# Loading a 268 MB matrix in tiles of 512 rows and three slots, instead of 384 rows and four slots

## The chip, the cores and the metric

The kernel runs on one core of one Trainium2 chip. The metric is the time of one execution on the device, in microseconds (us), the median of several executions. The kernel before takes 631.39 us (4 runs, 631.29 to 631.71). The runs come in batches; all kernels of one batch run on the same chip, each beside runs of the kernel before. The batches fell on different chips, and there the kernel before has medians between 631.36 and 632.11 us, so a kernel is compared with the runs of before of its own batch, or with a kernel of the same batch.

## The reference

```python
B, S, D = 8, 2048, 4096
proj = (x @ w).squeeze(-1)                 # x: (8, 2048, 4096) float32, w: (4096, 1)
cm = np.maximum.accumulate(proj, axis=1)
is_record = (proj >= cm).astype(np.float32)
return np.cumsum(is_record, axis=1).astype(np.float32)
```

One pass over x, 268.4 MB, decides everything. Each row of 4096 numbers (16 KB) becomes one dot product; a running maximum and a running count follow along each of the 8 sequences.

## The kernel before

Five groups of 384 positions are processed in a loop, and then one tail of 128 positions. In a group, each of the 8 sequences is one tile: 128 partitions with three consecutive rows each, so a tile is one load with one contiguous run of 48 KB per partition. Four slots of SBUF hold tiles. The loads are all issued from SyncE (SP) in program order; a load waits until its slot's last tile has been released (`fr`, counted by VectorE and ScalarE).

```python
    R = 3          # rows per partition and tile
    NS = 4         # slots
    NG = (S - P) // (R * P)                      # 5 groups
    ...
        for k in range(NK):                      # NK = NG * B = 40 tiles
            g, t = divmod(k, B)
            i = SY.dma_start(
                out=xbuf[k % NS],
                in_=x[B - 1 - t, g * N : (g + 1) * N, :].rearrange(
                    "(p r) d -> p (r d)", r=R
                ),
            ).then_inc(xs[k % NS], 16)
            if k >= NS:
                i._wait_ge(fr[k % NS], 2 * (k // NS))
```

Every row is split over three engines: VectorE multiplies and sums columns 0 to 2815 in one instruction, GpSimd (POOL) multiplies the other 1280 columns in place, ScalarE (ACT) sums those. Small matmuls transpose a group's sums into PSUM, and VectorE then runs three instructions over the group's positions: running maximum, comparison, running count.

```python
        with V.Fori(0, NG):                      # VectorE; POOL and ACT have the same loop
            group_scans()
            ...
            for t in range(B):
                b, s = B - 1 - t, t % NS
                V.wait_ge(xs[s], 16).then_inc(go, 1)
                V.sem_inc(xs[s], -16)
                for j in range(R):
                    i = dot(...)
                i.then_inc(fr[s], 1)
```

With four slots and eight tiles to a group, `k % NS` and `t % NS` are the same slot in every group. That is why the loop can be written once for all groups. The tail loads single 16 KB rows and, for the last sequences, narrow pieces.

## Time and profile before

| | before |
|---|---|
| time, median | 631.39 us |
| span of the profiled execution | 630.1 us |
| DMA, share of sixteen engines' span | 98.7% |
| VectorE, POOL, ACT busy | 64%, 59%, 28% |
| first load packet starts, last load has landed | 2.0 us, 623.57 us |

The page of the kernel before: the span; the DMA engines' mean busy share in tenths for forty slices; the DMA queues with packets, MB and share of sixteen engines' span; the engines on the chain that ended last; and the two costliest groups of instructions (busy us, mean ns of one, idle us before them and what ended it).

```profile
span 630.1 us, 1239 instructions
...
DMA  9999999999999999999999999999999999999995
...
q1 hardware_dynamic: 8016, 268.50, 98.7%
...
q14 instruction: 2, 0.02, 0.0%
...
POOL 52%; issue 38%; DMA 6%; PE 3%; DVE 0%; POOLq 0%; ACT 0%; SPq 0%; ACTq 0%
...
L120 DVE CUSTOM_DVE_ANT_0 xall<-xall,w_v 128x2816 f32<-128x2816 f32 (+3 forms) x135 | 389.3, 2931 | 185.8 <-DVEq L238 183.8
L252 POOL TENSOR_TENSOR xall<-xall,w_sb 128x1280 f32<-128x1280 f32 x120 | 345.2, 2903 | 246.0 <-POOLq L255 246.0
```

The chain is led by POOL and by "issue", but the last line shows POOL idle for 246.0 us: it waits for tiles. The limit is the load queue, in every slice but the last. The windows view of four tiles (columns: from and to, length, busy us of PE, PEld, DVE, ACT, POOL with counts, granted TensorE clock, DMA share, GB/s) says it best:

```profile
33.40:91.40 58.00, 0.00 (x0) 0.00 (x0) 36.45 (x24) 16.35 (x24) 34.51 (x12) 1.00 1.00 434
```

The DMA share is 1.00 and the rate 434 GB/s, while the busiest compute engine works 36.45 of 58.00 us. The Trainium skill, "DMA: Bandwidth & Descriptors", section Where 436 GB/s comes from, gives a ceiling of 435 GB/s for the sixteen DMA engines; this trace agrees. (The same section has the HBM side, at about 358 GB/s for a core, bind a load from HBM. Here this one core read at 434 GB/s, so that limit does not show, and the measurement decides.) So nothing that the compute engines do counts here, unless it makes the queue run dry.

`q14 instruction` are the fetches of the program itself.

The last three instructions of VectorE, in the timeline (start us, length us, instruction; in brackets the idle time before it and what ended that):

```profile
625.94 0.47 DVE L135 TENSOR_TENSOR_SCAN cm_l<-ps,cm,small 8x128 f32<-8x128 f32 x1 [1.70 <-PE ps L326]
626.45 0.28 DVE L139 TENSOR_TENSOR rec_l<-ps,cm_l 8x128 f32<-8x128 f32 x1
626.76 0.47 DVE L142 TENSOR_TENSOR_SCAN cnt_l<-rec_l,cnt,ps 8x128 f32<-8x128 f32 x1
```

More readings come from the trace's records and not from a view. A load's semaphore is counted up 16 times, which is read here as once by each DMA engine. The last of the 16 is called the landing here, and the time from the first to the last is the spread of the engines. In the kernel before, tiles land 14.50 us apart, tail rows 4.86 us apart, and the spread at the last landing is 1.36 us.

### The profile page before, as it was taken

To read this page: it belongs to the slowest core of one execution; us is meant where nothing else is said; L and a number is where in the kernel's file an instruction comes from. 1 tells how busy PE (TensorE), PEld (TensorE's weight loads), DVE (VectorE), ACT (ScalarE), POOL (GpSimd) and SP (SyncE) were. 2 spreads that over 40 slices of the span, in tenths; PEclk is the share of its full clock that TensorE was granted. 3 is DMA by queue.
4 is the path that set the end of the run, shared out by engine and by line. 5 is a ranking of instruction groups with operands and counts; after the bars stand their busy time and mean duration, and the time that the engine had idled before them with its cause. 6 is when DMAs were issued, how large, how long until landed. Compare 5 with 4: busy or idle time off the path is not lost.

```text
span 630.1 us, 1239 instructions
## 1 busy us (share of the span) xinstructions
PE 33.4 (5%) x100; PEld 14.7 (2%) x100; DVE 406.2 (64%) x295; ACT 177.7 (28%) x262; POOL 369.2 (59%) x137
## 2 busy tenths in 40 slices
PE   8000000010000001000000010000001000000103
PEld 3000000000000000000000000000000000000001
DVE  0756666677655557766666675556667766555886
ACT  1322223233232222233232322222232322322332
POOL 0555666666555555666666555556666665555864
PEclk9999999999999999999999999999999999999999
DMA  9999999999999999999999999999999999999995
GB/s 385 415 446 443 412 443 444 422 434 440 424 437 441 431 427 443 440 415 446 438 421 440 440 424 437 440 425 434 440 440 418 443 440 418 444 437 417 425 431 209
DMA packets 8035, 268.55 MB, mean 426 GB/s; under 512 B 936, under 2 KB 1496, under 8 KB 2016
## 3 DMA queue, kind: packets, MB, share of 16 engines
q1 hardware_dynamic: 8016, 268.50, 98.7%
q8 instruction: 1, 0.02, 0.0%
q10 hardware_dynamic: 16, 0.02, 0.0%
q14 instruction: 2, 0.02, 0.0%
HBM read 268.45 MB, written 0.07 MB: 426 GB/s over the span
## 4 chain that ended last, share of the span: by engine, by line
POOL 52%; issue 38%; DMA 6%; PE 3%; DVE 0%; POOLq 0%; ACT 0%; SPq 0%; ACTq 0%
POOL xall L252 52%; DMA xall<-in_x_dram 6%; PE w_v L206 2%; PE ps L326 1%; PE ps L206 0%; DMA w<-in_w_dram 0%; DVE xall L120 0%; POOLq L255 0%; ACT w L216 0%; DVE cm_l L135 0%; DVE cnt_l L142 0%; SPq L176 0%; DVE rec_l L139 0%; ACT xall L126 0%; POOLq L247 0%
## 5 line engine op out<-in xcount | busy, mean ns | idle before, releaser
L120 DVE CUSTOM_DVE_ANT_0 xall<-xall,w_v 128x2816 f32<-128x2816 f32 (+3 forms) x135 | 389.3, 2931 | 185.8 <-DVEq L238 183.8
L252 POOL TENSOR_TENSOR xall<-xall,w_sb 128x1280 f32<-128x1280 f32 x120 | 345.2, 2903 | 246.0 <-POOLq L255 246.0
L126 ACT ACTIVATE xall<-xall 128x1280 f32<-128x1280 f32 x129 | 162.6, 1261 | 430.9 <-POOL xall L252 413.1
L273 PE MATMUL ps<-identity,small 128*8 128x128 f32 x60 | 13.6, 418 | 567.1 <-ACT xall L126 567.1
L294 POOL TENSOR_TENSOR xall<-xall,w_sb 128x1280 f32<-128x1280 f32 (+1 forms) x8 | 22.1, 2765 | 6.7 <-DMA xall<-in_x_dram 6.6
L126 ACT ACTIVATION_READ_ACCUMULATOR xall<-xall 128x1 f32 x129 | 24.0, 186 | 0.0
L273 PEld LDWEIGHTS ps<-identity,small 128*8 128x8 f32 x60 | 7.4, 130 | 574.4 <-ACT xall L126 570.6
L135 DVE TENSOR_TENSOR_SCAN cm<-ps,cm,small 8x384 f32<-8x384 f32 x6 | 6.0, 1004 | 15.0 <-PE ps L273 15.0
L206 PE MATMUL w_v<-w,identity 8*128 8x512 f32 x14 | 12.1, 1056 | 0.0
L224 DVE MEMSET ps<- 8x384 f32 x1 | 0.4, 378 | 17.1 <-ACT w L216 17.1
L120 DVE DVE_READ_ACCUMULATOR2_ANT small<- 128x1 f32 x135 | 11.0, 81 | 0.0
L326 PE MATMUL ps<-identity,small 128*1 128x128 f32 (+1 forms) x24 | 5.7, 407 | 22.9 <-DVE small L120 22.8
L142 DVE TENSOR_TENSOR_SCAN cnt<-rec,cnt,ps 8x384 f32<-8x384 f32 x6 | 6.0, 1002 | 0.2
L206 PEld LDWEIGHTS w_v<-w,identity 8*128 8x128 f32 x14 | 4.7, 333 | 7.3 <-issue 7.3
L213 ACT COPY w_sb<-w_v 128x768 f32<-128x768 f32 x1 | 0.8, 799 | 11.4 <-PE w_v L206 11.4
L139 DVE TENSOR_TENSOR rec<-ps,cm 8x384 f32<-8x384 f32 x6 | 3.3, 546 | 0.2
L326 PEld LDWEIGHTS ps<-identity,small 128*1 128x1 f32 (+1 forms) x24 | 2.1, 108 | 26.5 <-DVE small L120 25.0
L206 PE MATMUL ps<-w,identity 8*128 8x512 f32 x2 | 2.1, 1136 | 2.6 <-DMA w<-in_w_dram 2.6
L212 ACT ACT_TABLE_LOAD x1 | 1.3, 1283 | 1.6 <-SPq L148 1.6
L135 DVE TENSOR_TENSOR_SCAN cm_l<-ps,cm,small 8x128 f32<-8x128 f32 x1 | 0.5, 471 | 1.7 <-PE ps L326 1.7
L212 ACT COPY w_sb<-ps 128x512 f32<-128x512 f32 x1 | 0.6, 586 | 1.9 <-PE ps L206 1.9
L294 POOL TENSOR_TENSOR xall<-xall,w 128x320 f32<-128x320 f32 x1 | 0.9, 870 | 0.1
(15 smaller groups left out, 3.4 us busy)
## 6 DMA issues: line engine op xcount, KB each, us to landing
xall<-in_x_dram SPq DMA_DIRECT2D x40, 6144.0 KB, 47.8
xall<-in_x_dram SPq DMA_DIRECT2D x6, 2048.0 KB, 42.7
xall<-in_x_dram SPq DMA_DIRECT2D x1, 1344.0 KB, 36.7
xall<-in_x_dram SPq DMA_DIRECT2D x2, 384.0 KB, 30.5
xall<-in_x_dram SPq DMA_DIRECT2D x1, 704.0 KB, 38.1
xall<-in_x_dram SPq DMA_DIRECT2D x1, 640.0 KB, 39.1
xall<-in_x_dram SPq DMA_DIRECT2D x1, 224.0 KB, 21.7
xall<-in_x_dram SPq DMA_DIRECT2D x1, 192.0 KB, 21.8
```

Source lines behind the costliest of these rows:

```text
L120: return V.tensor_tensor_reduce(out=xsl, in0=xsl, in1=wsl, scale=1.0, scalar=0.0, op0=ALU.mult, op1=ALU.add, accum_out=dst,)
L126: return A.activation(out=xsl, in_=xsl, func=ACTF.Copy, accum_out=dst)
L135: V.tensor_tensor_scan(out=cm_, data0=ps[:B, :n], data1=neg.to_broadcast([B, n]), initial=cm0, op0=ALU.max, op1=ALU.max,)._wait_ge(psr, ba ...
L139: V.tensor_tensor(out=rec_, in0=ps[:B, :n], in1=cm_, op=ALU.is_ge)._wait_ge(psr, base + 1).then_inc(psr, 1)
L142: V.tensor_tensor_scan(out=cnt_, data0=rec_, data1=zero.to_broadcast([B, n]), initial=cnt0, op0=ALU.add, op1=ALU.add,)._wait_ge(psr, base ...
L206: i = T.matmul(out=dst, lhsT=identity[:NW, k : k + 1].to_broadcast([NW, P]), rhs=w_row, start=True, stop=True,).then_inc(bw, 1)
L212: A.copy(out=w_sb[:, CV - VC :], in_=ps)._wait_ge(bw, 1).then_inc(wc, 1)
L213: A.copy(out=w_sb[:, : CV - VC], in_=w_v[:, VC:CV])._wait_ge(bw, NW).then_inc(wc, 1)
L252: i = G.tensor_mul(out=xl, in0=xl, in1=w_sb).then_inc(pl, 1)
L273: i = T.matmul(out=ps[:B, j:N:R], lhsT=l[:, j * B : (j + 1) * B], rhs=identity, start=k == 0, stop=k == 1,)
L294: G.tensor_mul(out=xl, in0=xl, in1=w_pool(*p))._wait_ge(landed, 16).then_inc(pl, 1)
L326: i = T.matmul(out=ps[:m, :P], lhsT=l[:, :m], rhs=identity, start=k == 0, stop=k == len(parts) - 1,)
```

## The change

Its intent is larger loads: four rows (64 KB) per partition and tile. Only three such slots fit. Three groups of 512 positions in a loop cover 1536 positions, then one group of 384-row tiles is written out after the loop, then the same tail. The comparison writes its flags over its input in PSUM, because their 2 KB no longer fit beside everything else in the SBUF. The core of the diff (cut):

```diff
-    R = 3
-    NS = 4
-    NG = (S - P) // (R * P)
+    RS = (4, 4, 4, 3)
+    R = RS[0]
+    NS = 3
+    NG = len(RS)
+    NL = NG - 1
...
-    xs = [sem("xs") for _ in range(NS)]
-    fr = [sem("fr") for _ in range(NS)]
+    xs = [sem("xs") for _ in range(B)]
+    fr = [sem("fr") for _ in range(B)]
...
         V.tensor_tensor(
-            out=rec_, in0=ps[:B, :n], in1=cm_, op=ALU.is_ge
+            out=ps[:B, :n], in0=ps[:B, :n], in1=cm_, op=ALU.is_ge
...
+    def user_before(g, t):
+        if t >= NS:
+            return t - NS, g + 1
+        return max(u for u in range(B) if u % NS == t), g
...
+        for g in range(NG):
+            r = RS[g]
+            for t in range(B):
+                i = SY.dma_start(
+                    out=xbuf[t % NS][:, : r * D],
...
+                ).then_inc(xs[t], 16)
+                u, n = user_before(g, t)
+                if n:
+                    i._wait_ge(fr[u], 2 * n)
...
-        with V.Fori(0, NG):
-            group_scans()
...
+        with V.Fori(0, NL):
+            next_group()
+            group_dots(R)
+        next_group()
+        group_dots(RS[-1])
```

A tile's slot is `t % NS`, its number within the group, so that the loop can still be written once.

More of the change, by code (lines that the diff above doesn't have):

```diff
@@ L41 @@
     NW = D // WC
-    R = 3
-    NS = 4
-    NG = (S - P) // (R * P)
+    RS = (4, 4, 4, 3)
[3 more added lines that the diff above has]
+    NL = NG - 1
     N = R * P
-    S0 = NG * N
-    assert S0 + P == S and B % NS == 0
+    STARTS = [sum(RS[:g]) * P for g in range(NG)]
+    S0 = sum(RS) * P
+    assert S0 + P == S
     VC = 2816
@@ L80 @@
     cm = sb([B, N], "cm")
-    rec = sb([B, N], "rec")
     cnt = sb([B, N], "cnt")
-    cm_l, rec_l, cnt_l = (sb([B, P], n) for n in ("cm_l", "rec_l", "cnt_l"))
+    cm_l, cnt_l = (sb([B, P], n) for n in ("cm_l", "cnt_l"))
     w_v = wpool.tile([P, CV], FP32, name="w_v")
@@ L100 @@
     neg = cut(1)[:B]
-    zero = ps[:B, WC - 1 :]
     ns = iter(range(1000))
@@ L132, in w_pool, with scans @@
         return w2[:, c0 - W2 : c1 - W2]
-    def scans(cm_, rec_, cnt_, n, cm0, cnt0, base=1):
+    def scans(cm_, cnt_, n, cm0, cnt0, base=1):
+        low = neg.to_broadcast([B, n])
         V.tensor_tensor_scan(
-            out=cm_, data0=ps[:B, :n], data1=neg.to_broadcast([B, n]), initial=cm0,
-            op0=ALU.max, op1=ALU.max,
+            out=cm_, data0=ps[:B, :n], data1=low, initial=cm0, op0=ALU.max, op1=ALU.max,
         )._wait_ge(psr, base).then_inc(psr, 1)
         V.tensor_tensor(
-            out=rec_, in0=ps[:B, :n], in1=cm_, op=ALU.is_ge
+            out=ps[:B, :n], in0=ps[:B, :n], in1=cm_, op=ALU.is_ge
@@ L141, in scans @@
         )._wait_ge(psr, base + 1).then_inc(psr, 1)
         V.tensor_tensor_scan(
-            out=cnt_, data0=rec_, data1=zero.to_broadcast([B, n]), initial=cnt0,
-            op0=ALU.add, op1=ALU.add,
+            out=cnt_, data0=ps[:B, :n], data1=low, initial=cnt0, op0=ALU.add, op1=ALU.max,
         )._wait_ge(psr, base + 2).then_inc(cs, 1)
-    NK = NG * B
+    def user_before(g, t):
+        if t >= NS:
+            return t - NS, g + 1
+        return max(u for u in range(B) if u % NS == t), g
@@ L148 @@
     with tc.tile_critical(no_gpsimd_drain=True):
-        for k in range(NK):
-            g, t = divmod(k, B)
-            i = SY.dma_start(
-                out=xbuf[k % NS],
-                in_=x[B - 1 - t, g * N : (g + 1) * N, :].rearrange(
-                    "(p r) d -> p (r d)", r=R
-                ),
-            ).then_inc(xs[k % NS], 16)
-            if k >= NS:
-                i._wait_ge(fr[k % NS], 2 * (k // NS))
-            if k == 0:
-                A.dma_start(
-                    out=w_row, in_=w.rearrange("(k c) one -> k (c one)", k=NW)
-                ).then_inc(ws, 16)
-            if t == NS and g:
-                SY.dma_start(
-                    out=out[:, (g - 1) * N : g * N], in_=cnt
-                )._wait_ge(cs, g + 1).then_inc(od, 16)
@@ L169, in slot @@
-        def slot(m):
-            return m // R, xbuf[m // R][:, (m % R) * D : (m % R + 1) * D]
-        freed = set()
+        for g in range(NG):
[3 more added lines that the diff above has]
+                    out=xbuf[t % NS][:, : r * D],
+                    in_=x[B - 1 - t, STARTS[g] : STARTS[g] + r * P, :].rearrange(
+                        "(p r) d -> p (r d)", r=r
+                    ),
+                ).then_inc(xs[t], 16)
+                u, n = user_before(g, t)
+                if n:
+                    i._wait_ge(fr[u], 2 * n)
+                if g == t == 0:
+                    A.dma_start(
+                        out=w_row, in_=w.rearrange("(k c) one -> k (c one)", k=NW)
+                    ).then_inc(ws, 16)
+                if t == 4 and g:
+                    SY.dma_start(
+                        out=out[:, STARTS[g - 1] : STARTS[g]], in_=cnt
+                    )._wait_ge(cs, g + 1).then_inc(od, 16)
@@ L174, in row_load @@
+        def slot(m):
+            if m < NS:
+                return None, xbuf[m][:, RS[-1] * D :]
+            u = B - NS if m < 2 * NS else B - NS + 1
+            return u, xbuf[u % NS][:, (m % NS) * D : (m % NS + 1) * D]
+        freed = {None}
         def row_load(m, c0, c1, b, done):
-            s, xb = slot(m)
+            u, xb = slot(m)
             i = SY.dma_start(
@@ L178, in row_load @@
             ).then_inc(done, 16)
-            if s not in freed:
-                freed.add(s)
-                i._wait_ge(fr[s], 2 * (NK // NS))
+            if u not in freed:
+                freed.add(u)
+                i._wait_ge(fr[u], 2 * NG)
         for m, b in enumerate(rows):
@@ L188 @@
                 SY.dma_start(
-                    out=out[:, (NG - 1) * N : S0], in_=cnt
+                    out=out[:, STARTS[-1] : S0], in_=cnt[:, : S0 - STARTS[-1]]
                 )._wait_ge(cs, NG + 1).then_inc(oe, 16)
@@ L223, with group_scans, group_dots @@
         V.wait_ge(wc, 3)
-        V.memset(ps[:B, :N], LOW)
-        V.memset(zero, 0.0).then_inc(psr, 1)
-        def group_scans():
+        V.memset(ps[:B, :N], LOW).then_inc(psr, 1)
+        def group_scans(r=R):
             V.wait_ge(od, 16)
-            scans(cm, rec, cnt, N, cm[:, N - 1 :], cnt[:, N - 1 :])
-        with V.Fori(0, NG):
-            group_scans()
-            V.sem_inc(psr, -3)
-            V.sem_inc(od, -16)
+            n = r * P
+            scans(cm[:, :n], cnt[:, :n], n, cm[:, N - 1 :], cnt[:, N - 1 :])
+        def group_dots(r):
             for t in range(B):
                 b, s = B - 1 - t, t % NS
-                V.wait_ge(xs[s], 16).then_inc(go, 1)
-                V.sem_inc(xs[s], -16)
-                for j in range(R):
+                V.wait_ge(xs[t], 16).then_inc(go, 1)
+                V.sem_inc(xs[t], -16)
+                for j in range(r):
                     i = dot(
@@ L243, with next_group, group_products @@
                     )
-                i.then_inc(fr[s], 1)
-        G.wait_ge(wc, 3)
-        with G.Fori(0, NG):
+                i.then_inc(fr[t], 1)
+        def next_group():
+            group_scans()
+            V.sem_inc(psr, -3)
+            V.sem_inc(od, -16)
+        with V.Fori(0, NL):
[3 more added lines that the diff above has]
+        group_dots(RS[-1])
+        def group_products(r):
             for t in range(B):
                 s = t % NS
-                for j in range(R):
+                for j in range(r):
                     xl = xbuf[s][:, j * D + VC : (j + 1) * D]
@@ L255, with group_sums @@
                 G.sem_inc(go, -1)
-        with A.Fori(0, NG):
+        G.wait_ge(wc, 3)
+        with G.Fori(0, NL):
+            group_products(R)
+        group_products(RS[-1])
+        def group_sums(r):
             for t in range(B):
                 b, s = B - 1 - t, t % NS
-                for j in range(R):
+                for j in range(r):
                     i = add_up(
@@ L264 @@
                     )._wait_ge(pl, j + 1)
-                i.then_inc(fr[s], 1)
-                A.sem_inc(pl, -R)
+                i.then_inc(fr[t], 1)
+                A.sem_inc(pl, -r)
             A.wait_ge(pd, 1)
             A.sem_inc(pd, -1)
-        for g in range(NG):
-            for j in range(R):
+        with A.Fori(0, NL):
+            group_sums(R)
+        group_sums(RS[-1])
+        for g, r in enumerate(RS):
+            for j in range(r):
                 for k, l in enumerate((sum_p, sum_v)):
                     i = T.matmul(
-                        out=ps[:B, j:N:R], lhsT=l[:, j * B : (j + 1) * B],
+                        out=ps[:B, j : r * P : r], lhsT=l[:, j * B : (j + 1) * B],
                         rhs=identity, start=k == 0, stop=k == 1,
@@ L277 @@
                     if j == k == 0:
-                        i._wait_ge(fr[NS - 1], 2 * (g + 1) * B // NS)
-                    if j == R - 1:
+                        i._wait_ge(fr[B - 1], 2 * (g + 1))
+                    if j == r - 1:
                         i.then_inc((pd, psr)[k], 1)
@@ L306 @@
             if m == 0:
-                group_scans()
+                group_scans(RS[-1])
         for i, (b, c0, c1, v, p) in enumerate(PIECES):
@@ L332 @@
         i.then_inc(psr, 1)
-        scans(cm_l, rec_l, cnt_l, P, cm[:, N - 1 :], cnt[:, N - 1 :], 4)
+        n = RS[-1] * P
+        scans(cm_l, cnt_l, P, cm[:, n - 1 : n], cnt[:, n - 1 : n], 4)
         SY.dma_start(out=out[:, S0:], in_=cnt_l)._wait_ge(cs, NG + 2).then_inc(oe, 16)
```

## The prediction

> **What bounds the kernel now.** The load of x. The page's busy slices: DMA at 9 tenths in all but the last; its queue table: 268.5 MB, 98.7% of sixteen engines' span. In the windows view, from 33.4 to 91.4 us (four tiles) the DMA share is 1.00 at 434 GB/s, with DVE busy 36.5 us and POOL 34.5 us of 58.0. The chain of waits names POOL (52%) and "issue" (38%), but POOL idles 246 us in all, about 5.8 us before every tile: it waits for landings. In the trace's packet records a 48 KB packet takes 1815 ns (27.1 GB/s per engine, 433 GB/s on sixteen), nearly always. The Trainium skill, "DMA: Bandwidth & Descriptors", section Where 436 GB/s comes from, gives a ceiling of 435 GB/s; the trace agrees, so the steady state is at its ceiling. Not transfer: about 2.0 us before the first packet and 6.7 us from the last landing (623.4) to the end.
>
> **What the change does.**
> - Tiles: 40 loads of 6 MiB become 24 of 8 MiB and 8 of 6 MiB; same bytes. Packets per engine fall by 64, completions by 8. Records of 16 KB (611 ns) and 48 KB (1815 ns) fit 36.7 ns per 1000 bytes plus 9 ns per packet, so 64 KB should take about 2417 ns (estimate). Saved: 72 x 9 ns = 0.65 us at most. Landings (14.50 us per tile, 4.86 us per 16 KB row) suggest an intercept of only 0.04 us a DMA, which saves 0.3 us. All of it is on the critical path.
> - Slots: three of 64 KB instead of four of 48 KB. A tile lands every 19.3 us (estimate); POOL's four products (4 x 2.88) and ACT's last sum (1.46) free it about 13 us after landing. When it is reissued, 6 us of the next tile and 19.3 us of the one after are still queued: 25 us of slack, against about 31 before. At a group's end 16 matmuls (12 took 2.73) and 512-wide scans (before 1.00 + 0.55 + 1.00 us at 384) delay the next tile 1 to 1.5 us; the slack swallows that. No queue gap.
> - Scans: three groups at 512 and one at 384, instead of five at 384; flags written in PSUM; the constant operand from PSUM to SBUF. Only the last 128-wide ones (0.47 + 0.28 + 0.47 us) are on the path; within 0.1 us of before.
> - The tail has the same pieces in the same order. Its first rows use free fourth rows and are issued earlier, into a full queue: worth nothing.
>
> **Prediction.** 631.44 - 0.4 = 631.0 us; 8 in 10: 630.1 to 632.2. Faster by over 2%: 0.01; within 2%: 0.96; slower by over 2%: 0.03.
>
> **What would show it.** DMA share 1.00 at 434 GB/s over full tiles; 64 KB packets near 2417 ns; POOL's idle time near 7.8 us before each tile (19.3 - 11.5); DVE, POOL and ACT busy times within 2% of before; still 6.7 us after the last landing.
>
> **What would make it wrong.**
> - 64 KB packets split or at another rate. Halved, they add 128 packets per engine over before, about +1.2 us; in 16 KB parts about +4.6 us.
> - Sixteen engines now step by powers of two in HBM (64 KB per partition). The same page, section Latency and other measured facts, has the rate falling from 512 KiB pitch up (207 against 214 GB/s); no run here shows it at 64 KB, and the rows at 16 KB pitch lose nothing.
> - Three slots running dry, were a tile freed 25 us later than I reckon; that would repeat per tile and cost percents.

## The result, and the profile after

The changed kernel takes 632.59 us (4 runs, 632.22 to 633.04) against 631.39: slower by 1.2 us, and above the range of 630.1 to 632.2. Ratios in this document are the mean time of one kernel's fast runs over that of the other's of the same rounds, so they are not quite the ratio of the medians quoted. Here the ratio is 1.0016 (95% interval 1.0002 to 1.003). The change was repeated twice in other batches: 1.0013 (0.9999 to 1.0026) and 1.0031 (1.0018 to 1.0044).

The same parts of the page, after:

```profile
span 631.0 us, 1174 instructions
...
DMA  9999999999999999999999999999999999999995
...
q1 hardware_dynamic: 6848, 268.50, 98.7%
...
q14 instruction: 4, 0.03, 0.0%
...
POOL 52%; issue 37%; DMA 6%; PE 3%; DVE 0%; POOLq 0%; ACT 0%; SPq 0%; ACTq 0%
...
L121 DVE CUSTOM_DVE_ANT_0 xall<-xall,w_v 128x2816 f32<-128x2816 f32 (+3 forms) x135 | 388.7, 2931 | 188.5 <-DVEq L244 186.5
L268 POOL TENSOR_TENSOR xall<-xall,w_sb 128x1280 f32<-128x1280 f32 x120 | 344.8, 2905 | 247.5 <-POOLq L271 247.5
```

Nothing on this page explains a loss: same shares, same busy times, the load queue busy in every slice. Two things differ, the packets (6848 instead of 8016) and the instruction fetches (4 instead of 2 within the span). The three last VectorE instructions are as before, so the flags in PSUM cost nothing there:

```profile
627.12 0.47 DVE L137 TENSOR_TENSOR_SCAN cm_l<-ps,cm,small 8x128 f32<-8x128 f32 x1 [1.63 <-PE ps L351]
627.63 0.29 DVE L140 TENSOR_TENSOR ps<-ps,cm_l 8x128 f32<-8x128 f32 x1
627.95 0.47 DVE L143 TENSOR_TENSOR_SCAN cnt_l<-ps,cnt,small 8x128 f32<-8x128 f32 x1
```

The whole chain before them is about as long, too. What moved is the last landing, from 623.57 to 624.85 us. So the question is where the load queue lost 1.3 us. The landings of all loads, one after the other, answer it (from the trace's records; us between landings):

```
before, 384-row tiles:              14.46 to 14.56, all 39 gaps of the 40 tiles
after,  512-row tiles:              19.28 to 19.46, but 19.85 once (100.33 to 120.18)
after,  first 384-row tile:         14.50   (467.95 to 482.45)
after,  second 384-row tile:        16.06   (482.45 to 498.51)
after,  the other 384-row tiles:    14.48 to 14.56
```

One gap is 1.56 us too long, at the step from the last 512-row group to the 384-row group. The windows view of the changed kernel, one window in mid-run (332.66 to 351.96) and three around the step:

```profile
332.66:351.96 19.30, 0.00 (x0) 0.00 (x0) 12.68 (x9) 5.45 (x8) 11.48 (x4) 0.52 1.00 435
467.95:482.45 14.50, 1.43 (x7) 0.92 (x8) 12.12 (x8) 5.45 (x8) 11.50 (x4) 0.50 1.04 427
482.45:498.51 16.06, 2.16 (x11) 1.10 (x8) 12.23 (x9) 4.09 (x6) 8.63 (x3) 0.50 0.93 398
498.51:513.00 14.49, 0.00 (x0) 0.00 (x0) 9.11 (x6) 4.09 (x6) 8.63 (x3) 0.50 1.00 434
```

In the third line the DMA share is 0.93 and the rate 398 GB/s. (A slice's packets are counted where they start, so the line before shows 1.04.) The granted TensorE clock is 0.50 from about 333 us on, but PE is busy 5% of the span, and the tail's matmuls took 5.64 us against 5.71 before. It plays no part.

Why the queue was short of work is in SP's timeline, the issues of loads:

```profile
422.96 0.33 SPq L157 DMA_DIRECT2D xall<-in_x_dram  x1
...
461.69 0.33 SPq L157 DMA_DIRECT2D xall<-in_x_dram  x1
...
481.00 0.80 SPq L157 DMA_DIRECT2D xall<-in_x_dram  x2
...
497.05 0.33 SPq L157 DMA_DIRECT2D xall<-in_x_dram  x1
```

The load at 422.96 is the last tile (t = 7) of the last 512-row group. Between that and 461.69 nothing is issued for 38.7 us, which is two tiles' time. The load at 461.69 is t = 0 of the next group: it wants slot 0, which t = 6 has just left. Then SP waits again, until 481.00, for slot 1, which t = 7 leaves 13.05 us after it landed at 467.95. Right behind it, in the same line, goes t = 2, whose slot 2 had been free since about 442 us: it stood behind t = 1 in SP's program order. So from 467.95, when t = 7 had landed, to 481.00 the queue held one load where three slots could have held two. With 64 KB tiles in the loop, that one load is 19.3 us of work and covers the 13 us. At the last step it is a 48 KB tile of 14.5 us, of which 14.5 - 13.05 = 1.45 us were left until its landing. A landing is the last engine's. In the packet records 14 of the 16 engines have moved their last byte of t = 0 by 481.66, at least 0.8 us before the landing at 482.45, and the first packets of t = 1 start only at 481.95, 0.95 us after the issue; 14 engines have theirs by 482.16, the other two by 482.60. From 481.66 to 481.95 only two engines are busy. The restarted engines' first packets then take 2.2 to 3.4 us instead of 1.815, as the very first ones of a run do (2.1 to 3.7 us in the kernel before). One coincidence has to be ruled out: an instruction fetch falls into the long gap, at 491.6 us. In run f3 below no fetch comes after 165 us, and the gap is still 16.10 us; in e1b a fetch comes at 492.0, and the gap is 14.52.

### The profile page after: what moved, and what is told of

It reads as the page before. It is cut to its first block, busy times and chain, and to the rows that moved or that the text cites. A ratio compares the mean times of both kernels' runs of the same rounds, so it can differ in the third digit from the quotient of the medians.

```text
span 631.0 us, 1174 instructions
## 1 busy us (share of the span) xinstructions
PE 33.1 (5%) x100; PEld 14.9 (2%) x100; DVE 406.0 (64%) x291; ACT 177.7 (28%) x262; POOL 368.9 (58%) x137
## 3 DMA queue, kind: packets, MB, share of 16 engines
q1 hardware_dynamic: 6848, 268.50, 98.7%
## 4 chain that ended last, share of the span: by engine, by line
POOL 52%; issue 37%; DMA 6%; PE 3%; DVE 0%; POOLq 0%; ACT 0%; SPq 0%; ACTq 0%
POOL xall L268 52%; DMA xall<-in_x_dram 6%; PE w_v L215 2%; PE ps L351 1%; PE ps L215 0%; DMA w<-in_w_dram 0%; DVE xall L121 0%; POOLq L271 0%; ACT w L225 0%; DVE cm_l L137 0%; DVE cnt_l L143 0%; SPq L185 0%; DVE ps L140 0%; ACT xall L127 0%; POOLq L274 0%
## 5 line engine op out<-in xcount | busy, mean ns | idle before, releaser
L137 DVE TENSOR_TENSOR_SCAN cm<-ps,cm,small 8x512 f32<-8x512 f32 (+1 forms) x5 | 6.1, 1218 | 13.5 <-PE ps L298 13.5
L143 DVE TENSOR_TENSOR_SCAN cnt<-ps,cnt,small 8x512 f32<-8x512 f32 (+1 forms) x5 | 6.1, 1217 | 0.2
L140 DVE TENSOR_TENSOR ps<-ps,cm 8x512 f32<-8x512 f32 (+1 forms) x5 | 3.3, 660 | 0.2
```

The source lines that it names most:

```text
L137: V.tensor_tensor_scan(out=cm_, data0=ps[:B, :n], data1=low, initial=cm0, op0=ALU.max, op1=ALU.max,)._wait_ge(psr, base).then_inc(psr, 1)
L140: V.tensor_tensor(out=ps[:B, :n], in0=ps[:B, :n], in1=cm_, op=ALU.is_ge)._wait_ge(psr, base + 1).then_inc(psr, 1)
L143: V.tensor_tensor_scan(out=cnt_, data0=ps[:B, :n], data1=low, initial=cnt0, op0=ALU.add, op1=ALU.max,)._wait_ge(psr, base + 2).then_inc(cs, 1)
```

## The experiments

The theory that the trace suggests, A: the queue runs dry at the last group step, because the slots do not rotate on there. The rivals: B, reads at steps of 64 KB, or packets of 64 KB, cost; C, the flags in PSUM or three slots as such cost. A fourth, D, came out of the first batch: the change makes the program longer, and the DMA engines that load x also fetch the program. Table of all runs, by batch; a line of dashes separates them.

| run | edit | median us | before in the batch | ratio |
|---|---|---|---|---|
| e1_rotate | slots rotate on at the last step | 632.04 | 631.89 | 1.0001 |
| e2_three_48k | three slots, 48 KB | 631.87 | 631.89 | 1.0002 |
| e3_delay_t7 | release of each group's last tile 2.8 us later | 637.45 | 631.89 | 1.0095 |
| e4_delay_t3 | the same for the fourth tile | 633.13 | 631.89 | 1.0021 |
| — | | | | |
| after_again | the change itself | 633.27 | 632.11 | 1.0013 |
| e5_unroll_before | before, loops written out | 633.49 | 632.11 | 1.0021 |
| e6_loop_48k | e2, all groups in the loop | 631.70 | 632.11 | 0.9997 |
| e7_flags_sbuf | e1, flags in SBUF, x moved | 633.74 | 632.11 | 1.0020 |
| — | | | | |
| e8_trim | e1, 28 fewer VectorE instructions | 631.38 | 631.59 | 0.9998 |
| e1b_rotate | e1 again | 631.68 | 631.59 | 1.0003 |
| e9_flags_sbuf | e1, flags in SBUF, x not moved | 631.43 | 631.59 | 0.9999 |
| e10_base | e1, x 896 bytes lower | 633.16 | 631.59 | 1.0028 |
| — | | | | |
| f1_after | the change itself | 633.45 | 631.36 | 1.0031 |
| f2_rotate | e1 | 632.16 | 631.36 | 1.0007 |
| f3_trim_only | the change, fewer VectorE instructions | 633.16 | 631.36 | 1.0021 |
| f4_both | e8 | 631.02 | 631.36 | 0.9990 |

Each interval is about 0.0013 to each side of its ratio, so single ratios near 1 are not told apart; the traces are.

### e1: let the slots rotate on at the last step

```diff
+        if g == NL:
+            return B - NS + t, g
         return max(u for u in range(B) if u % NS == t), g
+    def off_of(g):
+        return (B % NS) * (g == NL)
...
-                    out=xbuf[t % NS][:, : r * D],
+                    out=xbuf[(t + off_of(g)) % NS][:, : r * D],
```

The three compute loops of the last group, and the tail's slots, are moved by the same two slots. The last group is outside the loop anyway, so this needs no more instructions.

> The changed kernel, but the last group starts in the slot that was freed first (slots continue to rotate at the step from 512-row to 384-row groups). Theory A (at that step the second 48 KB tile waits for the slot of the tile before last-but-one to be freed, 13 us after it landed, with only 14.5 us of queue in front: the queue runs dry): the second tile of the last group lands 14.5 us after the first instead of 16.06, no slow first packets near 482 us, total 1.5 us less than the changed kernel, 631.0 us (630.6 to 631.5). Rival B (reads at 64 KB steps, or 64 KB packets, are what costs): the gap may close but the total stays at 632.2 or more. Rival C (flags in PSUM or the longer scans): stays at 632.2 or more.

Measured: the gap closed. The second tile lands 14.50 us after the first, and no packet is slow near 482 us. The total fell by less than expected: ratio 1.0001 against 1.0016 and 1.0013 of the change in other batches, that is 0.8 to 0.95 us instead of 1.5, and level with before rather than below it. So A names a real loss, but something took back part. By the time alone B is hardly excluded (632.04, where B was to leave 632.2 or more); the closed gap, and f1 against f2 on one chip below, put it out as the main cause. The repeat, e1b, in the windows and SP views:

```profile
467.80:482.30 14.50, 1.42 (x7) 0.92 (x8) 12.12 (x8) 5.45 (x8) 11.49 (x4) 0.50 1.00 434
482.30:496.80 14.50, 2.16 (x11) 1.10 (x8) 12.23 (x9) 4.02 (x6) 8.63 (x3) 0.50 1.00 434
496.80:511.30 14.50, 0.00 (x0) 0.00 (x0) 9.11 (x6) 4.16 (x7) 8.63 (x3) 0.50 1.00 434
```

```profile
442.24 0.33 SPq L162 DMA_DIRECT2D xall<-in_x_dram  x1
...
461.54 0.33 SPq L162 DMA_DIRECT2D xall<-in_x_dram  x1
...
480.85 0.33 SPq L162 DMA_DIRECT2D xall<-in_x_dram  x1
```

The loads of the last group are now issued one per released slot: at 442.24 one more load than before, and two are always queued. The DMA share stays 1.00 at 434 GB/s.

In e1's landings another gap stands out: one tail row lands 5.83 us after the row before it, where 4.86 is normal, while the first of the 16 engines keeps its pace (4.88). The spread steps from 1.35 to 2.30 us there. An 8 KB instruction fetch starts at 603.0 us. The kernel before has no fetch so late. This is theory D. The packet records of e1b show how: on one engine the fetch runs from 602.41 to 602.72, where the next packet of x should have started, and that packet then takes 1141 ns instead of 611. Together this is 0.84 us.

### e2: three slots without the larger tiles

```diff
-    RS = (4, 4, 4, 3)
+    RS = (3, 3, 3, 3, 3)
```

The slots keep a fourth row's room for the tail.

> Three slots and the changed slot order, but five groups of 384 rows with 48 KB per partition as in the kernel before. Theory A: a 48 KB tile is freed about 10.2 us after landing, with 14.5 us of queue in front of its successor, so 4 us are left at each group's end: no dry queue, every tile 14.5 us, 631.4 us as before (631.1 to 631.8). Rival C (three slots or flags in PSUM as such cost): over 632 us. Rival B (64 KB): 631.4 as well; it is e1 that tells B from A.

Measured: 631.87 us (just above the range expected), ratio 1.0002, and no gap at any group's end: tiles land 14.46 to 14.58 us apart, but 14.80 and 15.00 once each, within a group and next to an instruction fetch. Three slots with the group's own numbering, and flags in PSUM, show no cost when the tile in front is as long as the tile to be released. Rival C is out for these two.

### e3 and e4: a later release, at the step and in mid-group

ScalarE repeats its last sum of tile t = 7 (e3) or t = 3 (e4) twice before it releases the tile; the results are unchanged.

```diff
+                if t == 7:                       # 3 in e4
+                    for n in range(2):
+                        i.then_inc(dl, 1)
+                        i = add_up(...)._wait_ge(dl, n + 1)
+                    A.sem_inc(dl, -2)
                 i.then_inc(fr[t], 1)
```

> The changed kernel with two more ACT sums (about 3 us) before the last tile of each 512-row group is released. Theory A: the queue is already dry at the step to the 384-row group, so all 3 us are added there, and nothing at the two other group ends (19.3 us of queue against 16 us): second tile of the last group lands about 19 us after the first, total about 635.6 us (634.8 to 636.3). Rivals B and C: slot release has slack everywhere, within 0.5 us of the changed kernel.

> Control: the same 3 us before the release of the fourth tile of each 512-row group, where two tiles are queued. Theory A and the rivals: no effect, 632.6 us (632.0 to 633.1).

Measured: e3 takes 637.45 us (ratio 1.0095), 4.3 us more than e4 of the same batch (633.13). That is just above e4's range (633.1), but e4's ratio, 1.0021, lies within the three of the changed kernel (1.0013 to 1.0031), which did not run in this batch. Both delay one release per group by 2.8 us (174.60 against 171.83 at the first group's end). In mid-group that is free: after the first 121 us e4's 512-row tiles land 19.29 to 19.40 us apart, as in the changed kernel. At the group's end it is not. The windows of e3 at the step:

```profile
469.17:483.79 14.62, 0.00 (x0) 0.00 (x0) 12.12 (x8) 7.00 (x11) 11.49 (x4) 0.50 0.86 373
483.79:502.41 18.62, 3.58 (x16) 2.03 (x16) 12.23 (x9) 5.27 (x8) 8.62 (x3) 0.50 0.92 381
```

The second tile now lands 18.62 us after the first, 2.56 more than in the changed kernel. That is the dose-response that A asks for. One expectation missed: at the first group's end, where I had counted on slack, the gap grew too, by about 1.05 us (20.36 against 19.30). There the load was issued at 174.60. Two of the 16 engines ended their queued packets at 176.80 and 176.93 and started the next ones only at 177.23 and 178.10, and one of these took 4.0 us. So a margin of about 2.2 us between an issue and the end of an engine's queue is not always enough. At the second group's end the last landing lost nothing, but the mean of the engines did. In these means e3 loses 0.24, 0.54 and 3.20 us more than the changed kernel at the three group ends. That is 3.98 of the 4.04 us by which its third tail row lands later (603.56 against 599.52), so the expectation failed in the main at the two earlier group ends, which have less slack than I had counted on.

### e5 and e6: the length of the program

e5 is the kernel before with its three loops written out:

```diff
-        with V.Fori(0, NG):
+        for _ in range(NG):
```

(the same for POOL and ACT). e6 is e2 with its last group back in the loop.

> The kernel before with its three loops over the groups written out, nothing else changed. Theory D (a longer program is fetched in more 8 KB pieces by one of the DMA engines that load x; each piece puts that engine 0.4 to 1.0 us behind the others, so the last landing comes later): more than two fetches while x is loaded, perhaps seven, the spread between the first and the last engine at the last landing grows from 1.36 us by 0.3 us or more per extra fetch, and the time by as much, 1.5 to 3 us in all (ratio 1.0025 to 1.005). Rival (fetches cost nothing, or fall on different engines): spread below 2 us, ratio within 0.001 of 1.

> Run e2 (three slots of 48 KB) with its last group back in the loop, so the program is as short as before. Theory D: two fetches during the load instead of three, no step of 0.5 us in the spread of landings near 517 us, spread at the last landing about 1.0 us instead of 1.5; time 0.3 to 0.5 us below e2, too small for the times to settle. Rival: same spread as e2.

Measured for e5: ratio 1.0021 (1.0007 to 1.0035), slower by 1.4 us (just under the range expected), with six fetches during the load instead of two:

```profile
q14 instruction: 6, 0.05, 0.0%
```

The spread of the engines at the landings, with the fetches (trace's records; us):

```
fetch at   109.9  119.0  182.2  313.9  380.7  532.3
spread     0.95 to 1.35 (up to 309)  ->  2.0 (324 to 527)  ->  3.0 (543 to the last landing)
```

The first engine of the 16 finished the last load at 622.35, as in the kernel before (622.21); the last one at 625.35 (before 623.57). So the loads as a whole are not slower, one engine is. The spread grows by 1.0 us at 313.9 and again at 532.3, by 0.4 at 119.0, and not at 109.9, 182.2 and 380.7. My expectation of a step at every fetch was wrong. The three fetches at 109.9, 313.9 and 532.3 come when VectorE has started 67, 191 and 323 recorded instructions, 124 and 132 apart; the other ones fit ScalarE (58 and 187) and POOL (64). So VectorE's fetches, which slow one packet of x by 0.53 us where the others slow one by 0.21 to 0.25, seem to be the ones that hit the engine that is last; that assignment is inferred from the counts.

Measured for e6: two fetches as before, spread 0.89 us at the last landing against 1.50 in e2, which had a third fetch at 516.7. The time, ratio 0.9997 against e2's 1.0002, is as expected too small a difference to count.

### e7, e9 and e10: the flags, and a confounded run

> Run e1 with the flags written to SBUF again instead of in place in PSUM (a scratch tile is made smaller to have the room). All theories: off the critical path except for the last 128 columns; the three last DVE instructions 0.47, 0.28, 0.47 us either way, time within 0.3 us of e1 (ratio 1.000, 0.999 to 1.001).

The flags need 2 KB of SBUF that was not all there, so e7 made an unused scratch tile smaller:

```diff
-    small = sb([P, 352], "small")
+    small = sb([P, 128], "small")
+    rec = sb([B, N], "rec")
...
-            out=ps[:B, :n], in0=ps[:B, :n], in1=cm_, op=ALU.is_ge
+            out=rec[:, :n], in0=ps[:B, :n], in1=cm_, op=ALU.is_ge
```

Measured: 633.74 us, ratio 1.0020, against e1's 1.0001, and not within 0.3 us of it. Tiles land 19.35 us apart instead of 19.31, rows 4.89 instead of 4.85. Packets of 16 KB take 615 ns instead of 611, packets of 5 KB 201 instead of 196 (medians). The edit had also moved x, and what is allocated after it, 896 bytes down in SBUF, by the order of the allocations. Two runs part the two:

> Run e1 with the flags in SBUF as in the kernel before, and x at the same SBUF address as in e1 (run e7 had moved it by 896 bytes). If e7's loss of 1.6 us came from the address: as e1, ratio 1.000 (0.999 to 1.001), tiles 19.31 us and rows 4.85 us apart. If flags in SBUF cost it: ratio 1.002, tiles 19.35 and rows 4.89 us apart.

> Run e1 with x 896 bytes lower in SBUF and nothing else changed (flags stay in PSUM). If e7's loss came from the address: tiles 19.35 us and rows 4.89 us apart as in e7, ratio 1.002 (1.001 to 1.003). If from the flags: as e1, ratio 1.000.

e9 has the flags in SBUF and x where it was (the running maximum of the tail reuses part of the flags' tile). e10 has only the smaller scratch tile. Measured: e9 ratio 0.9999, rows 4.85 us apart; e10 ratio 1.0028, rows 4.89 us apart, 16 KB packets 615 ns in the median. So the move by 896 bytes costs 1.5 us (633.16 against 631.68 of e1b in the same batch), and the flags show no cost. Rival C is out for the flags as well. The change itself does not move x.

### e8: take the late fetch away

```diff
-                V.wait_ge(xs[t], 16).then_inc(go, 1)
-                V.sem_inc(xs[t], -16)
+                if r == R:                       # in the loop only
+                    V.wait_ge(xs[t], 16).then_inc(go, 1)
...
+                    if r < R and j == 0:         # last group: the first dot waits itself
+                        i._wait_ge(xs[t], 16)
```

POOL takes the count back in the loop and waits for the landing itself in the last group. Two more counts are not taken back at all, and two waits are merged into memsets. VectorE's stream is 28 instructions shorter.

> Run e1 with 28 fewer instructions in VectorE's stream (no semaphore counts taken back in the last group, the per-tile count in the loop taken back by GpSimd). Theory D: VectorE's second 8 KB fetch, at 603 us in e1, falls after the loads or away; the spread of the engines' last landing stays near 1.2 us instead of stepping from 1.3 to 2.3, the row that landed 5.83 us after the one before in e1 lands after 4.86, the last landing is 1 us earlier (623.6) and the time 0.6 to 1.0 us below e1, ratio to before 0.9985 to 0.9990: the fastest of all. Rival (fetches cost nothing): as e1, ratio 1.000.

> Run e1 again, to be compared with e8, e9 and e10 on the same chip: ratio 1.000 (0.9995 to 1.0008), a fetch near 603 us with a step of 1 us in the spread of landings.

Measured: e8's fetches come at 117.3, 124.6 and 165.6 us, and none later. The row at 604 us lands 4.88 us after the one before it (e1b: 5.84), and the spread stays at 1.2 us (e1b: 1.98). The time is 631.38 us against 631.68, a gain of 0.3 us and not the 0.6 to 1.0 expected, and within the scatter of the runs (630.86 to 631.88 against 631.47 to 632.03). The fetch at 492 us of e1b is gone as well, but it had made no step in the spread. In the profiled execution of e8, bursts of packets slowed by about 0.1 us stretched the early gaps (to as much as 19.96 us), 1.1 us more in sum than in e1b. I have no cause for such bursts. Counted as stretches of 2.5 us with eight or more packets over 40 ns too long, outside the starts and the group ends, they are in 10 of the 14 profiled runs with 64 KB packets and in one of the four with 48 KB (e6, at 118 us). Whether the larger loads bring them was not tested. If they do, they can eat the saving that the change was to bring.

### f1 to f4: both repairs, crossed, on one chip

Two questions were left: what the dry queue is worth in the total, and whether the late fetch counts in the changed kernel itself. f2 is e1, f4 is e8, f3 is e8 without the rotation.

> The changed kernel, as the corner without either repair, on the same chip as f2 to f4: ratio 1.0014 (1.0010 to 1.0018).

> Slots rotate on (as e1), long program. Dry queue removed: 0.8 to 1.1 us below f1, ratio 1.0001 (0.9998 to 1.0004); the full 1.5 us of the gap is not seen because the engine behind by two fetches is then the last.

> Dry queue kept, shorter VectorE stream (as e8). In the changed kernel's traces the late fetch moved the last landing by only 0.1 to 0.25 us, since the restart after the dry queue had just evened the engines out: 0.1 to 0.4 us below f1, ratio 1.0010 (1.0006 to 1.0013). If the fetch were the main cause in the changed kernel: near 1.0000.

> Both repairs (as e8): 0.3 to 0.8 us below f2, ratio 0.9995 (0.9990 to 0.9999). If the fetch cost nothing: as f2.

Measured (medians, us):

| | long program | shorter VectorE stream |
|---|---|---|
| queue runs dry | 633.45 (f1) | 633.16 (f3) |
| slots rotate on | 632.16 (f2) | 631.02 (f4) |

The rotation is worth 1.3 us with the long program and 2.1 us with the short one. The short program is worth 0.3 us while the queue runs dry and 1.1 us once it does not. The gain of the rotation is clear of the scatter in both columns: the fastest run of f1 (632.53) is slower than the slowest of f2 (632.38), and the fastest of f3 (632.12) slower than the slowest of f4 (631.41). The gain of the short program is so in the lower row alone (f2's fastest 631.45). Expected were 0.8 to 1.1 us between f1 and f2 and 0.3 to 0.8 between f2 and f4; both came out larger. The ratio of f1, 1.0031, lies above what was expected, and so do the ratios of f2 and f3; the runs of before in this batch fall into two heaps, 631.07 to 631.36 and 631.85 to 632.60, so the differences among f1 to f4 are the better reading. The last landings tell much the same story, but in the single executions profiled the stretch from the last landing to the end scatters too, from 5.2 to 6.6 us over all runs:

```
                     before   f1       f2       f3       f4
third row, mean      598.17   599.75   597.98   599.77   597.71    mean of the 16 engines
last landing         623.57   625.06   624.26   625.07   623.17
spread there           1.36     0.93     1.98     1.01     1.29
```

The means of the 16 engines at the third tail row (before the late fetch) show the dry queue without the fetch: 1.77 us between f1 and f2, of which 1.47 is the gap itself (16.00 against 14.53 in the mean). The fetch then adds 1.0 us to the spread in f2. In f1 it adds little to the last landing (5.07 against 4.86, 0.21 us): perhaps the restart at 482 us left the engine that the earlier fetches had held back no longer far behind the others, so that the late fetch only just makes it the last. This is not shown: the records do not name the engines, and e4, with the same dry queue (a gap of 15.99 us), did lose 1.0 us at its late fetch (a row of 5.90 us, spread 1.01 to 2.04). That the two repairs are worth more together than apart, by 0.8 us in the medians, is within the scatter of the runs.

f4 has the fastest median of its batch, 631.02 us against 631.36, ratio 0.9990 (0.9977 to 1.0003); its other run, e8, gave 0.9998. It is faster than the change, and with before it is level within the interval. Its queue table, and its windows at the step:

```profile
q14 instruction: 3, 0.02, 0.0%
```

```profile
467.80:482.30 14.50, 1.40 (x7) 0.92 (x8) 12.12 (x8) 5.45 (x8) 11.51 (x4) 1.00 1.00 434
482.30:496.80 14.50, 2.18 (x11) 1.10 (x8) 12.21 (x9) 4.09 (x6) 8.60 (x3) 0.71 1.00 434
```

## Why the prediction was right or wrong

- **What bounds the kernel: right.** The DMA share is 1.00 at 434 GB/s before, and 1.00 at 435 GB/s over a full 512-row tile after.
- **Packets: right in the rate, the saving not shown.** 64 KB packets take 2418 ns, against 2417 predicted, and 512-row tiles land 19.31 us apart. Of the saving of 0.4 us there is no clear sign: in the six runs with the dry queue away and x in place, the third tail row lands at 597.71 to 598.70 in the mean of the engines (f4, e1b, f2, e1, e9, e8), against 598.17 in the one profile of before.
- **Slots: wrong, and this is the step that failed.** The prediction said of a freed tile: "6 us of the next tile and 19.3 us of the one after are still queued: 25 us of slack", and "No queue gap." That holds in mid-group (e4: a delay of 2.8 us there costs nothing). It counted the slots as a rotation of three. But a tile's slot is its number in the group modulo 3, and 8 is not a multiple of 3, so at a group's end only one load is queued. The slack there is the length of that load less 13 us: 6.3 us between 512-row groups, and 1.45 us at the step to 384 rows. Of this the issue takes 0.95 us to reach the first engine, and 14 of the engines have run out 0.8 us or more before the landing. The queue ran dry and lost 1.5 us. The program showed this: the lines of `user_before` say which tile each load waits for, and the list of SP's instructions has the order.
- **The program's own fetches: missing from the prediction.** The group written out after the loop adds two 8 KB fetches during the load. In three profiles of the changed kernel the late one costs 0.2 to 0.3 us of the last landing, in e4 1.0 us; with the queue repaired it costs about 1 us (e1, e1b, f2).
- **The sum.** Predicted -0.4; measured +1.2. The last landing moved by 1.28 us (623.57 to 624.85): the dry queue's +1.5, less 0.2 for everything else. That rest is not the packets' gain measured: the mean of the engines moved by 1.35 us up to the third tail row (598.17 to 599.52), and the spread there was smaller (0.89 against 1.36) before the late fetch added its part. The bullet that named the danger, "Three slots running dry", was right about the danger, and put it 25 us away.
- **Scans and flags: right.** The three last instructions take 0.47, 0.29 and 0.47 us against 0.47, 0.28 and 0.47, and e9 shows no difference in time. The wait before them did not grow.
- **The tail: right in substance.** From the last landing to the end it took 6.56 us before and 6.17 after, within the scatter over all runs.
- **The large steps in HBM: no loss at 64 KB.** The skill's figure for a pitch of 512 KiB ("DMA: Bandwidth & Descriptors", Latency and other measured facts) was named as a risk. Here a packet read at a pitch of 64 KB runs at 27.1 GB/s per engine, as at 48 KB (the bursts under e8 aside).

## What to carry to other kernels

When a loop's buffers are numbered within the iteration, check the seam: if the tiles of one iteration are not a multiple of the slots, the load that waits for the youngest tile stands in front of one whose slot is free, and the queue is one load short there. Compute the slack of a queue at each seam, and where the tile size changes, from the shortest load that stands alone in it, less the time from landing to release and from issue to first packet. Reckon to the engine that finishes first, and leave some microseconds over (2.2 us were not enough for two engines in one case here). When the DMA engines are the limit, count what else they carry, the program included, and look at the last of the sixteen engines and not at their mean.

## What the Trainium skill lacked or had wrong

- "Runtime: NRT & Kernel Launch", section Instruction fetch mechanics: it says that crossing a block boundary is "mostly hidden" and that the program is refilled in 16 KiB blocks. It speaks of the engine that runs the program. Here the records of the instruction queue show packets of 8192 bytes, about 128 of VectorE's recorded instructions apart (67, 191, 323). They are not hidden from the load of x, which is the limit: two of them, VectorE's by the counts, put one DMA engine 1.0 us behind the others each (spread 1.1 to 2.0 to 3.0 us in e5).
- The same section says that kernels prefer full unrolling where possible. Writing out the loops of the kernel before cost 1.4 us (ratio 1.0021, 1.0007 to 1.0035).
- "DMA: Bandwidth & Descriptors", section Latency and other measured facts, gives about 0.6 us to the first byte of a load. Here it is 0.95 us from the start of the issuing instruction to the first packet and 0.62 us from its end (it takes 0.33 us), so the figure agrees if it counts from the end, which the page does not say. What the page does not have: after a pause the engines' first packets take 2.2 to 3.4 us instead of 1.815, so that a queue empty for under a microsecond lost 1.5 us.
- "SBUF — State Buffer" says nothing of a destination address that slows a DMA at 128 partitions. Here x, and what is allocated after it, 896 bytes lower in SBUF made packets 4 to 5 ns longer (16 KB: 611 to 615 ns; 5 KB: 196 to 201 ns) and the kernel 1.5 us slower (e10 against e1b).
- No page has the bursts of packets slowed by about 0.1 us on most engines at once, which cost 1.1 us more in one execution (e8) than in another (e1b), and which are in 10 of the 14 profiled runs here with 64 KB packets and in one of the four with 48 KB. Their cause stays open.
